# Eight instead of seven units of the down projection with seven products; where their block sums are made and loaded

## The chip, the cores and the metric

The kernel runs on one core of one Trainium2 chip. The metric is device time in microseconds, the median of several executions. The engines are TensorE (PE in the profile; its weight loads are PEld), VectorE (DVE), ScalarE (ACT), GpSimd (POOL) and SyncE (SP). Transfers between HBM and the on-chip memory are issued from the queues of SP, ACT and POOL. Three executions before the change took 295.79, 296.03 and 296.15 us, median 296.03.

## The reference

One layer of a decoder, 256 tokens of width 1024, all in float32:

```
h   = rmsnorm(x, ln1_g)
z   = h @ w_in                      # 1024 x 2824
mix = concat[pool_mixer(z), mlstm(z), attention(z)]
x   = x + mix @ w_out               # 1024 x 1024
h2  = rmsnorm(x, ln2_g)
u   = causal_dwconv3(h2 @ w_up)     # 1024 x 5632
x   = x + (silu(u[:, :2816]) * u[:, 2816:]) @ w_down   # 2816 x 1024
```

The change touches the last line. The input of the down projection, a = silu(gate) * value, has 2816 = 22 x 128 columns. The kernel takes them in 11 units of 256, so a unit is the product of a 256 x 256 part of a (tokens by columns) and a 256 x 1024 part of w_down.

## The kernel before, in words

**Precision.** Each product of float32 operands is made of three passes on TensorE. An operand is split into a high part (ScalarE copies it to the reduced type, ACT `Copy`) and a low part (VectorE subtracts the high part from the full one). Then high x high, high x low and low x high are summed in PSUM. So every block of weights costs a turn of ScalarE and a turn of VectorE before TensorE can use it.

**Units.** All weights come as units of 128 x 2048 numbers (1 MB): 11 for the input projection, 4 for the output projection, 22 for the up projection (one per pair of 128 gate and 128 value columns), 11 for the down projection (U_DOWN + 0 to 10). `load` (L187) issues a unit's transfer on SP's queue. There are four rotating buffers, and two more from the up stage on, and a transfer is issued when the low part of an earlier unit has been taken from its buffer (`load_next`, L206). High and low parts have four buffers each (HL_BUFS).

**Plain and seven-product units.** A plain down unit is 2 x 2 x 2 blocks (two token halves, two column halves of a, two halves of the 1024 outputs), three passes each: 24 matmuls of 128 x 128 x 512. The units in SEVEN (2 to 8) are computed by Strassen's scheme in Winograd's form: seven products instead of eight, 21 matmuls (`down_seven`, L1315). For it a unit needs, besides three of its four weight blocks (1536 columns, loaded as such), four sums of weight blocks (2048 columns, a second load), and four differences of blocks of a (`diffs`, L1233: three subtractions on VectorE, in place in `a_sv`). All of these are split in high and low parts too (`sums`, L1332); the differences' parts lie in `h_2`, which the up stage no longer needs (tile h in the profile). `combine` (L1369) brings the seven accumulators together at the end.

**Block sums.** The sums of weight blocks are made by the transfers themselves, in HBM (tiles `far`): for each unit three plain copies of blocks and then three transfers that add a block to what is there (`far_step`, L1216). An addition has to wait until what it adds to and what it adds has landed. All six are issued on GpSimd's queue, for one unit after the other, with the next unit's copies issued while an addition is under way (L1223 to L1231). The finished sums are loaded as a unit's second transfer. `far_gate`, a small copy on GpSimd, holds back the steps of later units until the high part of the first up unit is there.

**Order of work.** The order on each engine is written by hand. Up to the second norm a table (PLACE) sets it. In the up loop (L1246) pass i issues TensorE's matmuls of up unit i, and for ScalarE and VectorE the work on unit i - 1: `up_sum` (z), the three taps of the convolution, the gate, the split of a; between them, the split of the weight units two and three further on, and one entry of a list `late`. Its last entries are the differences of the first EARLY = 5 seven-product units; the other two units' differences are made in the down stage. After the loop the last pair's work is issued (L1388), with the preparation of the first seven-product unit between it. Then the down loop (L1406) issues the preparation of unit i + 1 or so ahead of the products of unit i. The two units LAST (9, 10) come last, in an order that lets the outputs leave early.

Of the kernel before, what the change touches and what calls it, by code (L numbers as in the profile page):

```python
# [37 lines left out]
SEVEN = (2, 3, 4, 5, 6, 7, 8)  # L38
EARLY = 5
# [101 lines left out]
def kernel(  # L141
# [42 lines left out]
    s_far, s_raw = {}, {}  # L184
    later = [(U_DOWN + i, x) for i in range(N_DOWN) for x in range(1 + (i in SEVEN))]

    def load(u, at=None):  # L187
# [16 lines left out]
        nc.sync.dma_start(raw[:, :n], src)  # L204

# [57 lines left out]
    nc.sync.dma_start(con, consts)  # L263
# [136 lines left out]
    def next_loads():  # L400
        load(RAW_BUFS - 1)
        for t in range(NT):
            nc.sync.dma_start(xs[:, t], x[t * P:(t + 1) * P])
        load(RAW_BUFS)
# [727 lines left out]
    a_hi = fpool.tile([P, NPAIR, S], F32R, name="a_hi")  # L1132
    a_lo = fpool.tile([P, NPAIR, S], F32R, name="a_lo")
# [49 lines left out]
    def up_last(i):  # L1183
        for j in range(2):
            n = 10 + 2 * i + j
            y_t[i, j] = one(f"fy{i}{j}") if i > 1 else a_sv[:, n, :]
            nc.scalar.activation(y_t[i, j], up_t[i][j], AF.Copy, scale=pcol(Q_FC + i + NPAIR * j + 4 * NPAIR))  # L1187
# [18 lines left out]
    def up_out_hi(i):  # L1206
        n = P if i in slot and i % 2 == 0 else S
        nc.scalar.activation(a_hi[:, i, :n], y_t[i, 1][:, :n], AF.Copy)  # L1208

    def up_out_lo(i):  # L1210
        n = P if i in slot and i % 2 == 0 else S
        nc.vector.tensor_sub(a_lo[:, i, :n], y_t[i, 1][:, :n], a_hi[:, i, :n].bitcast(F32))

    for i in SEVEN:
        s_far[i] = dpool.tile([P, 4, 512], F32, name=f"far{i}")
    def far_step(i, n):  # L1216
        b = w[U_DOWN + i].rearrange("p (b c) -> p b c", c=512)
        at, src, block = ((slice(0, 1), b, 0), (slice(1, 3), b, 2), (slice(3, 4), b, 1), (slice(0, 2), b, 3),
                          (slice(2, 3), s_far[i], 0), (slice(3, 4), s_far[i], 2))[n]
        nc.gpsimd.dma_start(s_far[i][:, at, :], src[:, block:block + 1, :].to_broadcast([P, at.stop - at.start, 512]),  # L1220
                            **({"accum_op": ALU.add} if n > 2 else {}))

    far_steps = [[(i, n) for n in range(3)] for i in SEVEN]  # L1223
    far_steps = [*far_steps[0], (SEVEN[0], 3), *far_steps[1], (SEVEN[0], 4), None, (SEVEN[0], 5),
                 *(x for m, i in enumerate(SEVEN) if m
                   for x in ((i, 3), *(far_steps[m + 1] if m + 1 < len(SEVEN) else ()), (i, 4), (i, 5)))]
    for x in far_steps:
        if x:
            far_step(*x)
# [16 lines left out]
    for i in range(2, NPAIR):  # L1246
        u, m = U_UP + i, i - 1
        up(i, 0)
        if i == 2:
            up_rows_t(0)  # L1250
            up_rows_t(1)
        up(i, 1)
        if i == 2:
            split(u + 2, 0)
            split(u + 2, 1)
            split_hi(u + 3, 0, 2)
            split_hi(u + 3, 1, 2)
            continue
        more = u + 3 < U_DOWN + 2
        *first, last = late.pop(0) if i > 3 and late else (None,)  # L1260
        first += [None] * (2 - len(first))
        up_sum(m)
        if more:
            split_hi(u + 3, 0, 2)
        if u + 2 < U_DOWN + 2:
            split_lo(u + 2, 0, 2)
        up_last(m)
        if more:
            split_hi(u + 3, 1, 2)
        if first[0]:  # L1270
            first[0]()
        up_taps(m)
        if m > 2:
            up_out_lo(m - 1)
        if first[1]:
            first[1]()
        up_gate(m)
        up_out_hi(m)
# [243 lines left out]
```

## Time and profile before

| | us |
|---|---|
| median of three executions | 296.03 |
| profiled execution, its own time | 295.98 |
| its span | 294.2 |
| TensorE busy | 289.6 |
| VectorE busy | 259.6 |
| ScalarE busy | 209.2 |
| GpSimd busy | 45.1 |

A row of a group gives line, engine, operation, output tile and inputs with shapes, count, busy time and mean duration, and the idle time of the engine just before. A row of a timeline gives start, length, engine, line, operation and tiles; idle time before it and what ended it stand in brackets. Times are counted from the start of the span. A row of the chain gives start, length and what ran.

### The profile page before, as it was taken

The numbers are of one execution on the slowest core, as the hardware profiler recorded it, in microseconds if no ns is written. First come the engines' busy times: TensorE is split into PE (matmuls) and PEld (weight loads), VectorE is DVE, ScalarE is ACT, GpSimd is POOL, SyncE is SP. The second block draws the span as 40 slices with busy tenths as digits, with TensorE's granted clock in tenths as the row PEclk, the third lists the DMA queues.
The fourth block names the chain that finished last, engine by engine and source line by source line (L and its number), as shares of the span: only waits on it lengthen the run. The fifth ranks groups of instructions, "written<-read, shape, count | busy, mean of one in ns | idle before, by whom it ended". The sixth has DMA issues, their size and how long they took to land.

```text
span 294.2 us, 4572 instructions
## 1 busy us (share of the span) xinstructions
PE 289.6 (98%) x1609; PEld 246.3 (84%) x1609; DVE 259.6 (88%) x518; ACT 209.2 (71%) x395; POOL 45.1 (15%) x73
## 2 busy tenths in 40 slices
PE   8999999999999999999999999999999999999995
PEld 4999888788778788888888888988988988888884
DVE  2978998999987857769999999999999989999992
ACT  3868679679894736987787787687677478786700
POOL 1000104724100005105015105015102110000000
PEclk9999999999999999999999999999999999999999
DMA  7998874079976476999998998997988988998003
GB/s 258 416 419 304 347 290 164 2 158 319 206 283 256 175 285 234 192 319 339 276 367 211 296 341 211 329 339 186 334 273 185 284 218 271 350 313 354 1 1 143
DMA packets 16599, 75.39 MB, mean 256 GB/s; under 512 B 1844, under 2 KB 2240, under 8 KB 10688
## 3 DMA queue, kind: packets, MB, share of 16 engines
q1 hardware_dynamic: 9808, 59.24, 53.7%
q0 software_dynamic: 6048, 14.68, 24.9%
q10 hardware_dynamic: 720, 1.19, 1.1%
q8 instruction: 12, 0.20, 0.3%
q14 instruction: 11, 0.09, 0.1%
HBM read 74.04 MB, written 15.73 MB: 305 GB/s over the span
## 4 chain that ended last, share of the span: by engine, by line
PE 97%; DMA 2%; DVE 0%; SPq 0%; issue 0%
PE up L1170 25%; PE up L1173 13%; PE wo L885 8%; PE dn L885 6%; PE m L1294 6%; PE dn L1294 5%; PE of L511 2%; DMA head<-in_xt 2%; PE B L497 1%; PE V L497 1%; PE V L499 1%; PE V L498 1%; PE B L499 1%; PE upr L1103 1%; PE upr L1102 1%; PE B L498 1%
## 5 line engine op out<-in xcount | busy, mean ns | idle before, releaser
L221 DVE TENSOR_TENSOR lo<-raw,hi 128x1024 fp32r<-128x1024 f32 (+2 forms) x74 | 82.7, 1136 | 2.8 <-ACT hi L214 2.8
L1170 PE MATMUL up<-h,hi 128*128 128x512 f32 x320 | 76.3, 391 | 0.0
L214 ACT ACTIVATE hi<-raw 128x1024 fp32r<-128x1024 f32 (+2 forms) x74 | 71.0, 983 | 3.1 <-PE wo L885 1.6
L1170 PEld LDWEIGHTS up<-h,hi 128*128 128x128 f32 x320 | 58.9, 188 | 11.4
L1173 PEld LDWEIGHTS up<-h,lo 128*128 128x128 f32 x320 | 41.0, 191 | 1.5
L1173 PE MATMUL up<-h,lo 128*128 128x256 f32 x320 | 41.6, 283 | 0.0
L1191 DVE SCALAR_TENSOR_TENSOR fy<-z,par,fy 128x255 f32<-128x255 f32 (+1 forms) x80 | 33.2, 478 | 0.0
L1220 POOL DMA_DIRECT2D far<-far x14 | 11.8, 846 | 106.3 <-DMA far<-in_w 57.9
L1220 POOL DMA_DIRECT2D far<-in_w x28 | 23.0, 1256 | 7.5 <-DMA far<-in_w 7.5
L1187 ACT ACTIVATE fy<-z,par 128x256 f32<-128x256 f32 x40 | 18.1, 501 | 1.5 <-DVE z L1180 1.2
L1201 ACT ACTIVATE fy<-fy 128x256 f32<-128x256 f32 x20 | 8.4, 418 | 12.0 <-DVE fy L1191 12.0
L1180 DVE TENSOR_TENSOR z<-up,zl 128x512 f32<-128x512 f32 x20 | 13.8, 689 | 3.2 <-ACT zl L1178 2.9
L1178 ACT ACTIVATE zl<-up 128x512 f32<-128x512 f32 x20 | 11.9, 595 | 4.9 <-PE up L1173 4.9
L221 DVE TENSOR_TENSOR lo<-more_raw,hi 128x1024 fp32r<-128x1024 f32 x12 | 14.6, 1217 | 0.0
L1294 PE MATMUL m<-ph,h 128*128 128x512 f32 x42 | 14.1, 389 | 0.0
L214 ACT ACTIVATE hi<-more_raw 128x1024 fp32r<-128x1024 f32 x12 | 12.6, 1052 | 0.0
L1208 ACT ACTIVATE a_hi<-a_sv 128x256 fp32r<-128x256 f32 (+1 forms) x16 | 5.7, 369 | 8.1 <-DVE a_sv L1203 8.1
L885 PE MATMUL wo<-hi,mix_hi 128*128 128x512 f32 x32 | 11.2, 411 | 0.0
L1329 ACT ACTIVATE ph<-sum 128x1024 fp32r<-128x1024 f32 x8 | 8.4, 1055 | 3.1 <-PE dn L1294 2.3
L885 PE MATMUL wo<-lo,mix_hi 128*128 128x512 f32 x32 | 10.6, 393 | 0.0
L885 PE MATMUL wo<-hi,mix_lo 128*128 128x512 f32 x32 | 10.6, 392 | 0.0
L1330 DVE TENSOR_TENSOR pl<-sum,ph 128x1024 fp32r<-128x1024 f32 x8 | 9.8, 1220 | 0.0
(331 smaller groups left out, 644.4 us busy)
## 6 DMA issues: line engine op xcount, KB each, us to landing
raw<-in_w SPq DMA_DIRECT2D x33, 1024.0 KB, 8.5
far<-in_w POOLq DMA_DIRECT2D x14, 512.0 KB, 12.2
more_raw<-in_w SPq DMA_DIRECT2D x6, 1024.0 KB, 8.7
sum<-far SPq DMA_DIRECT2D x4, 1024.0 KB, 6.9
far<-in_w POOLq DMA_DIRECT2D x14, 256.0 KB, 13.7
far<-far POOLq DMA_DIRECT2D x14, 256.0 KB, 7.2
more_raw<-far SPq DMA_DIRECT2D x3, 1024.0 KB, 8.1
raw<-in_w SPq DMA_DIRECT2D x4, 768.0 KB, 5.3
```

Of the source, the lines that this page charges most:

```text
L214: nc.scalar.activation(hi_t[u][:, s], raw_t[u][:, s], AF.Copy)
L221: nc.vector.tensor_sub(lo_t[u][:, s], raw_t[u][:, s], hi_t[u][:, s].bitcast(F32))
L885: nc.tensor.matmul(acc[t, c][:, :n], a, b[:, k, o:o + n], start=st and i == 0, stop=sp and i == 2)
L1170: nc.tensor.matmul(up_t[i][:, j], a, h_2[:, k].rearrange("p c t -> p (c t)"), start=k == 0, stop=False)
L1173: nc.tensor.matmul(up_t[i][:, j, :S], a, h_hi[:, k, :], start=False, stop=k == KT - 1)
L1178: nc.scalar.activation(zl, ps[:, :, S:], AF.Copy)
L1180: nc.vector.tensor_add(z, ps[:, :, :S], zl)
L1187: nc.scalar.activation(y_t[i, j], up_t[i][j], AF.Copy, scale=pcol(Q_FC + i + NPAIR * j + 4 * NPAIR))
L1191: nc.vector.scalar_tensor_tensor(y[:, d:], up_t[i][j][:, :S - d], pcol(Q_FC + i + NPAIR * j + 2 * NPAIR * tap), y[:, d:], op0=ALU.mult, op ...
L1220: nc.gpsimd.dma_start(s_far[i][:, at, :], src[:, block:block + 1, :].to_broadcast([P, at.stop - at.start, 512]), **({"accum_op": ALU.add} ...
L1294: nc.tensor.matmul(dst, a[x], b[y], start=start and n == 0, stop=stop and n == 2)
L1330: nc.vector.tensor_sub(l[:, s], src, h[:, s].bitcast(F32))
```

## The change

SEVEN gets unit 1, so eight units have seven products and units 0, 9 and 10 are plain. EARLY goes to 6, so that two units' differences stay in the down stage as before. The first seven-product unit's weights are now split in the last two passes of the up loop, where the plain unit 1 was split, and its sums and differences after it, in a new order of single steps.

The three copies of `far_step` for units 1 and 2 (AHEAD = 2) move to SP's queue, behind the loads of units 10 and 11 of the input and output projections. On GpSimd's queue, the additions of units 1 and 2 are issued alternately ahead of the gate; behind it come, in each round, the first addition of one unit, the second of the unit before and the third of the one before that, and then the copies of a next unit.

The constants' load moves from behind the parameters to behind unit 6's load, and the rows of x from behind unit 3's load to behind unit 14's. The tiles a_hi and a_lo leave out the 128 columns that seven-product units don't use.

```
SEVEN = (1, 2, 3, 4, 5, 6, 7, 8)        # was (2, ..., 8)
EARLY = 6                               # was 5
AHEAD = 2
...
    def load_rest(u):                   # called at the end of load(u)
        if u == 6:
            nc.sync.dma_start(con, consts)
        for i in SEVEN[:1] if u == N_IN - 1 else SEVEN[1:AHEAD] if u == N_IN else ():
            for n in range(3):
                far_step(nc.sync, i, n)
        if u == 14:
            for t in range(NT):
                nc.sync.dma_start(xs[:, t], x[t * P:(t + 1) * P])
...
    far_steps = [(SEVEN[m], n) for n in range(3, 6) for m in range(2)]
    far_steps.append(None)
    far_steps += [(SEVEN[2], n) for n in range(3)]
    for m in range(2, len(SEVEN) + 2):
        far_steps += [(SEVEN[m - n + 3], n) for n in (3, 4, 5) if 2 <= m - n + 3 < len(SEVEN)]
        if AHEAD <= m + 1 < len(SEVEN):
            far_steps += [(SEVEN[m + 1], n) for n in range(3)]
    for x in far_steps:
        if x:
            far_step(nc.gpsimd, *x)
...
    def sums(i):                        # now returns its steps by name
...
        for k in range(2):
            c = slice(768 * k, 768 * k + 768)
            add(f"w{k}", hi_t[u][:, c], lo_t[u][:, c], raw[:, c], 0 if k else None)
            c = slice(D * k, D * k + D)
            add(f"s{k}", p_hi[i][:, c], p_lo[i][:, c], s[:, c], 1 if k else None)
        add("d", *s_hl[i], a_sv[:, 2 * n:2 * n + 2, :].rearrange("p k t -> p (k t)"))
        return steps
...
    def prepare(i):
        if i in SEVEN:
            names = "w0hi w0lo w1hi w1lo s0hi s0lo dhi dlo s1hi s1lo".split()
            if SEVEN.index(i) >= EARLY:
                names = "d0 w0hi w0lo d1 w1hi w1lo d2 s0hi s0lo dhi dlo s1hi s1lo".split()
...
        def next_hi(part):              # in the up loop
            if u + 3 <= U_DOWN:
                split_hi(u + 3, part, 2)
            elif u + 3 == U_DOWN + 1:
                first[f"w{part}hi"]()
...
    m = NPAIR - 1
    up_sum(m)
    first["s0hi"]()
    first["s0lo"]()
    up_last(m)
    first["dhi"]()
    first["s1hi"]()
    up_taps(m)
    first["dlo"]()
    up_gate(m)
    up_out_hi(m)
    first["s1lo"]()
    up_out_lo(m - 1)
    up_out_lo(m)
...
    ready = 2                           # was 3
```

More of the change, by code (lines that the diff above doesn't have):

```diff
@@ L1131, with a_pair @@
     fpool = ctx.enter_context(tc.tile_pool(name="fpool", bufs=1))
-    a_hi = fpool.tile([P, NPAIR, S], F32R, name="a_hi")
-    a_lo = fpool.tile([P, NPAIR, S], F32R, name="a_lo")
+    starts, blocks_a = [], 0
+    for i in range(NPAIR):
+        starts.append(blocks_a)
+        blocks_a += 1 if i // 2 in SEVEN and i % 2 == 0 else 2
+    a_hi = fpool.tile([P, blocks_a, P], F32R, name="a_hi")
+    a_lo = fpool.tile([P, blocks_a, P], F32R, name="a_lo")
+    def a_pair(d, i):
+        return d[:, starts[i]:(starts + [blocks_a])[i + 1], :].rearrange("p b c -> p (b c)")
     a_sv = fpool.tile([P, 2 * len(SEVEN), S], F32, name="a_sv")
@@ L1206, in up_out_hi @@
     def up_out_hi(i):
-        n = P if i in slot and i % 2 == 0 else S
-        nc.scalar.activation(a_hi[:, i, :n], y_t[i, 1][:, :n], AF.Copy)
+        d = a_pair(a_hi, i)
+        nc.scalar.activation(d, y_t[i, 1][:, :d.shape[1]], AF.Copy)
     def up_out_lo(i):
[L1211 to L1226, printed above, removed]
+        h, d = a_pair(a_hi, i), a_pair(a_lo, i)
+        nc.vector.tensor_sub(d, y_t[i, 1][:, :d.shape[1]], h.bitcast(F32))
+    far_steps = [(SEVEN[m], n) for n in range(3, 6) for m in range(2)]
[5 more added lines that the diff above has]
+            far_steps += [(SEVEN[m + 1], n) for n in range(3)]
     for x in far_steps:
         if x:
-            far_step(*x)
+            far_step(nc.gpsimd, *x)
         else:
@@ L1244 @@
     late += [diffs(i) for i in SEVEN[:EARLY]]
[L1246 to L1278, printed above, removed]
-        if u + 2 < U_DOWN + 2:
-            split_lo(u + 2, 1, 2)
-        if last:
-            last()
-    assert not late
     LAST = (N_DOWN - 2, N_DOWN - 1)
@@ L1312, in down @@
                 acc[t, c] = aux([P, 512], f"dn{t}{c}")
-        rows_product(U_DOWN + i, (a_hi, a_lo), 2 * i, i == span[0], i == span[1], t, cs, sub=sub)
+        lhs = [d[:, starts[2 * i]:starts[2 * i] + 4, :].rearrange("p (k b) c -> p k (b c)", k=2) for d in (a_hi, a_lo)]
+        rows_product(U_DOWN + i, lhs, 0, i == span[0], i == span[1], t, cs, sub=sub)
     def down_seven(i):
```

109 lines of the change are left out of this document (68 added, 41 removed).

## The prediction

> **What bounds the kernel now.** I read the page first, then the chain of waits, then the stretches of the down stage, then VectorE's order of time there.
>
> ```profile
> span 294.2 us, 4572 instructions
> PE 289.6 (98%) x1609; PEld 246.3 (84%) x1609; DVE 259.6 (88%) x518; ACT 209.2 (71%) x395; POOL 45.1 (15%) x73
> ...
> PE 97%; DMA 2%; DVE 0%; SPq 0%; issue 0%
> ```
>
> TensorE carries 97% of the chain. Nothing that only starts a transfer earlier can shorten this, and fewer matmuls can, if their inputs come in time. The chain in order of time, over the down stage (start, length, what):
>
> ```profile
> 235.44 10.91 PE dn L885 x48
> 246.35 0.68 PE m L1294 x3
> ...
> 274.91 0.68 PE m L1294 x3
> ...
> 279.67 8.16 PE dn L885 x36
> ```
>
> Two plain units (0 and 1) take 10.91 us for 48 matmuls, 0.227 each. Seven units with seven products run from 246.35 to 279.67: 33.32 / 7 = 4.76 us for 21 matmuls. No wait stands between them. Next, who is nearly as busy, in the stretch of one unit (its ends, length, PE, PEld, DVE, ACT, POOL, clock, DMA share, GB/s):
>
> ```profile
> 265.40:270.10 4.70, 4.70 (x22) 3.88 (x22) 4.70 (x8) 3.89 (x5) 0.00 (x0) 1.00 1.00 417
> ```
>
> In this stretch of 4.7 us VectorE has no free time, and ScalarE has 0.8. So VectorE's order of time decides whether fewer matmuls are worth anything:
>
> ```profile
> 232.34 1.22 DVE L221 TENSOR_TENSOR lo<-raw,hi 128x1024 fp32r<-128x1024 f32 x1
> 233.48 1.66 DVE L1191 SCALAR_TENSOR_TENSOR fy<-z,par,fy 128x255 f32<-128x255 f32 x4
> 235.05 0.42 DVE L1212 TENSOR_TENSOR a_lo<-fy,a_hi 128x256 fp32r<-128x256 f32 x1
> ...
> 236.86 0.69 DVE L1180 TENSOR_TENSOR z<-up,zl 128x512 f32<-128x512 f32 x1
> ...
> 240.84 0.42 DVE L1203 TENSOR_TENSOR fy<-fy,fy 128x256 f32<-128x256 f32 x1
> 242.69 1.23 DVE L1330 TENSOR_TENSOR pl<-more_raw,ph 128x1024 fp32r<-128x1024 f32 x1 [1.44 <-ACT ph L1329]
> 243.84 0.69 DVE L277 TENSOR_TENSOR h<-a_sv,h 128x512 fp32r<-128x512 f32 x1
> 244.44 1.22 DVE L1330 TENSOR_TENSOR pl<-more_raw,ph 128x1024 fp32r<-128x1024 f32 x1
> ...
> 264.69 0.42 DVE L898 TENSOR_TENSOR a_sv<-a_sv 128x256 f32<-128x256 f32 x1
> 265.02 0.95 DVE L1344 TENSOR_TENSOR lo<-raw,hi 128x768 fp32r<-128x768 f32 x1
> 265.89 0.29 DVE L898 TENSOR_TENSOR a_sv<-a_sv 128x128 f32<-128x128 f32 x1
> 266.09 0.95 DVE L1350 TENSOR_TENSOR lo<-raw,hi 128x768 fp32r<-128x768 f32 x1
> ...
> 273.65 0.68 DVE L277 TENSOR_TENSOR h<-a_sv,h 128x512 fp32r<-128x512 f32 x1
> ...
> 287.87 0.69 DVE L1384 TENSOR_TENSOR xs<-dn,xs 128x512 f32<-128x512 f32 x1 [0.87 <-PE dn L885]
> ...
> 290.73 0.42 DVE L1384 TENSOR_TENSOR xs<-tail,xs 128x256 f32<-128x256 f32 x1 [1.01 <-PE tail L885]
> ```
>
> From start to start this gives prices on a busy VectorE: a low half of 1024 columns 1.14 us (232.34 to 233.48), of 768 0.87 (265.02 to 265.89), of 512 0.60 (243.84 to 244.44), four taps 1.57, a 256-column step 0.33 (264.69 to 265.02), a 128-column difference 0.20 (265.89 to 266.09). Preparing a unit with seven products costs 2 x 0.87 + 2 x 1.14 + 0.60 = 4.62 us, just under TensorE's 4.76. The differences of a unit add 0.33 + 2 x 0.20 = 0.73, and a unit that carries them in the down stage costs 5.35, so there VectorE falls behind by 0.59. Units 7 and 8 carry them, before and after. From 232 to 287 its only hole is the 1.44 us at 242.69. Brackets give the idle time before an instruction and what ended it.
>
> **The change, part by part.** *TensorE.* Unit 1 goes from 24 matmuls to 21: 10.91 / 48 x 3 = 0.68 us less. This is the whole gain, from inputs in time.
>
> *VectorE.* Its work ahead of the last down units grows. Removed: unit 1's split, 2 x 1.14 = 2.28. Added: unit 1 as a seven-product unit, 4.62; one more set of differences (EARLY 6, in the last pass of the up loop), 0.73. The new order of the last block (the second unit's work no longer between the gates) fills the hole: from 240.84 + 0.33 to 242.69 it was 1.52 us. It opens a small one: the last z now starts at 236.86 + 0.73 - 2 x (1.14 - 0.87) = 237.05 and ends its turn at 237.65, and the low half of the first sums then waits for its high half on ScalarE:
>
> ```profile
> 236.17 0.58 ACT L1178 ACTIVATE zl<-up 128x512 f32<-128x512 f32 x1
> 236.65 0.83 ACT L1343 ACTIVATE hi<-more_raw 128x768 fp32r<-128x768 f32 x1
> ...
> 243.09 1.05 ACT L1329 ACTIVATE ph<-more_raw 128x1024 fp32r<-128x1024 f32 x1
> ```
>
> zl moves with the gate ahead of it by 0.26 (differences 0.53 less one saved 0.27), so the high half starts at 236.17 + 0.26 + 0.48 = 236.91, ends 1.05 later, and VectorE starts at about 238.00: a hole of 0.35. Sum: 4.62 + 0.73 + 0.35 - 2.28 - 1.52 = 1.90, less some 0.05 for small holes in the old block: VectorE is 1.85 us later at unit 8.
>
> What is late then? The third product of a unit needs the low half of the differences (the 0.60 step, tile h) as weights of its third matmul. Old times on TensorE (weight loads, then a matmul):
>
> ```profile
> 276.33 0.19 PEld L1294 LDWEIGHTS dn<-hi,h 128*128 128x128 f32 x1
> ```
> ```profile
> 276.56 0.39 PE L1294 MATMUL dn<-hi,h 128*128 128x512 f32 x1
> ```
>
> Before, that low half was done at 273.65 + 0.68 = 274.33, 2.00 us ahead of the weight load at 276.33. After, it is done at 276.18, and TensorE, 0.68 earlier, would want it at 275.65: 0.53 late. How a weight load that waited is followed by its matmul is seen once, at the start (VectorE, weight load, matmul):
>
> ```profile
> 4.32 0.35 DVE L390 TENSOR_SCALAR h_f<-head 128x256 f32<-128x256 f32 x1 [4.32 <-DMA head<-in_xt]
> ```
> ```profile
> 4.73 0.96 PEld L511 LDWEIGHTS of<-head,h_f 128*128 128x128 f32 x4 [0.36 <-DVE h_f L390]
> ```
> ```profile
> 5.05 1.04 PE L511 MATMUL of<-head,h_f 128*128 128x260 f32 x4
> ```
>
> 0.06 from VectorE's end to the load, 0.32 from load to matmul, where the steady spacing is 0.23. So the matmul that started at 276.56 starts at 276.18 + 0.06 + 0.23 to 0.32 = 276.47 to 276.56. Of the 0.68 gained, 0 to 0.09 are left at this point. I take 0.09, the steady spacing, since the matmul before it still runs there. [...]
>
> Earlier units by the same chain. In unit 2 the low half of the differences follows 237.05 by the rest of the last block, 0.60 + 0.35 + 1.14 + 1.57 + 0.60 + 0.33 + 1.14 + 2 x 0.33 = 6.39 (z, the hole, first sums, taps, differences, gate, second sums, two token halves), then 1.74 + 1.14 of its own: it starts at 246.32 and is done at 247.01. Unit 8 wanted its weights at 276.33, which is 1.42 after its place 274.91 in the chain; unit 2's place is now 235.44 + 5.46 + 4.76 = 245.66, so it wants them at 247.08: 0.07 to spare, about the size of what the reading leaves open. Then VectorE gains 0.14 a unit up to unit 6 and loses 0.59 in unit 7, which comes out about even, and 0.59 in unit 8. So one stall, at unit 8. If unit 2 or 7 stalls too, unit 8's shrinks by as much, because the end is VectorE's either way. Behind it the block sums are in time: VectorE makes the first ones ahead of the differences; the second ones are done 0.60 + 1.22 - 0.69 = 1.13 later and wanted eight matmuls, 1.81, later. The tail has room for VectorE's 1.85: it waits for TensorE 0.87 us at 287.87 and 1.01 at 290.73.
>
> *Transfers.* Loads are issued by freed buffers, and in the down stage the order slips by one place.
>
> ```profile
> far<-in_w POOLq DMA_DIRECT2D x14, 512.0 KB, 12.2
> ...
> sum<-far SPq DMA_DIRECT2D x4, 1024.0 KB, 6.9
> ```
>
> The third load from here, the sums of unit 5, is the closest. It goes out when unit 2's last low half is done, 246.32 + 0.60 + 1.22 = 248.14. VectorE takes unit 5's first sums three preparations on, at 243.44 + 3 x 4.62 + 1.74 = 259.04, and ScalarE needs 1.05 before that, 258.0: 9.8 us for a landing of 6.9. Early on, the constants go behind unit 6's load (20.11), the block copies of units 1 and 2 behind those of units 10 and 11 (45.72), the x rows behind unit 14's (77.61):
>
> ```profile
> 20.11 0.33 SPq L204 DMA_DIRECT2D raw<-in_w  x1
> ```
> ```profile
> 45.72 0.33 SPq L204 DMA_DIRECT2D raw<-in_w  x1
> ```
> ```profile
> 77.61 0.33 SPq L204 DMA_DIRECT2D raw<-in_w  x1
> ```
> ```profile
> 66.34 1.04 ACT L214 ACTIVATE hi<-raw 128x1024 fp32r<-128x1024 f32 x1
> ```
> ```profile
> 239.35 0.81 POOL L1220 DMA_DIRECT2D far<-far  x1 [5.73 <-DMA far<-far]
> ```
>
> Unit 11's load at 45.72 has 20.6 us until it is used at 66.34; three copies ahead of it and three behind, at 12.2 each group, fit. The constants and the x rows are first used here:
>
> ```profile
> L558 DVE TENSOR_TENSOR gm<-gm,con x2: 416/416/417, 45.6 to 45.9; 128x256 f32<-128x256 f32 x2
> ```
> ```profile
> L895 DVE TENSOR_TENSOR xs<-wo,xs x4: 680/682/694, 104.8 to 112.5; 128x512 f32<-128x512 f32 x4
> ```
>
> From 20.11 to 45.6 and from 77.61 to 104.8 there are 25 us and more. I cost all of these at nothing, and no gain either, because TensorE waits for nothing in that part; without that cover each is worth at most one landing, 12.2. GpSimd's last add stood at 239.35; three units side by side take one wait a round where two stood, so it comes no later, against sums wanted only at about 262.
>
> Sum: -0.68 + 0.59 = -0.09. The profiled execution took 295.98 with a span of 294.2; the median is 296.03. So 296.03 - 0.09 = 295.94.
>
> **The rivals.** *A, the whole gain:* VectorE is at least 0.5 us earlier than my chain, for instance if the new block order leaves no hole (0.35) and its gate runs as early as before (0.19). Then 296.03 - 0.68 = 295.35. For it: the chain has some ten terms, each read to 0.05. Against: the rows repeat to 0.01 us from unit to unit. *B, slower:* a load lands late in the down stage. With leads down to 9.8 us, one landing of the 12.2 that the copies show is 2.4 us late on ScalarE, VectorE has no slack, and TensorE ends 2.4 us later than forecast: 298.35. It is slower than before by the bound below once a landing passes 9.8 + 0.59 + 0.09 = 10.5. For it: 417 GB/s at 265. Against: the adds then no longer run beside the loads. *C, the chain longer than figured* by 0.3 to 0.6 (a second hole in the last block): 296.25 to 296.55, still no change by the bound below.
>
> **How the numbers follow.** A measurement of this kernel tells 0.2%, 0.59 us, from no change. The forecast has 0.48, C 0.14 (both no change), A 0.24 (faster, and near the bound, so its weight is what the chain's reading leaves open), B 0.14 (slower). The likeliest alone spans 295.6 to 296.2. The range takes in A less the spread of the shown runs (0.15) below, 295.2, and C and a little of B above, 296.7; B's far end is the part left out.
>
> **What would show it.** Right: TensorE busy some 0.7 us less, one idle time of about 0.6 us before a matmul of the last seven-product unit, put down to VectorE's difference low half (tile h), VectorE without holes from 238 on. A would show no such idle time and an end 0.68 earlier. B would show ScalarE waiting for raw or sum. Wrong altogether: idle time on TensorE in the first 230 us.

## The result, and the profile after

The changed kernel takes 298.44 us (median of eight executions, 297.07 to 300.23) against 296.06 (295.79 to 296.31) for the kernel before on the same chip: a ratio of 1.0087, 95% interval 1.0063 to 1.0111. The forecast was 295.94, its range ended at 296.7: it is slower, and by none of the ways forecast. The profiled execution is the slowest of the eight (300.23), so its rows show where time went, in somewhat larger sizes than the median's 2.4 us.

The page of the changed kernel: its span, the engines' busy time, the shares of the chain.

```profile
span 298.5 us, 4590 instructions
PE 291.4 (98%) x1606; PEld 247.0 (83%) x1606; DVE 262.4 (88%) x524; ACT 210.4 (70%) x398; POOL 46.1 (15%) x73
PE 52%; DVE 31%; DMA 6%; issue 4%; ACT 4%; SPq 0%; DVEq 0%; ACTq 0%
```

Three matmuls fewer, as intended, but TensorE is no longer 97% of the chain. The chains in order of time say where. Before, then after: the first transfer, the first matmuls on it, the start of the up loop, the last step.

```profile
1.24 4.42 DMA head<-in_xt
6.36 6.40 PE of L511 x28
...
123.25 3.63 PE up L1170 x16
```
```profile
1.26 4.71 DMA head<-in_xt
6.66 6.40 PE of L530 x28
...
127.62 3.63 PE up L1197 x16
...
294.91 0.42 DVE xs L1362
```

The up loop starts 4.37 us later (127.62 against 123.25). From there to VectorE's last step the changed kernel takes 294.91 - 127.62 = 167.29, the one before 290.73 - 123.25 = 167.48: 0.19 less, where the forecast had 0.09 less. So the whole loss lies ahead of the up loop. The first matmuls start 0.30 later, behind a first transfer that took longer. The windows of the changed kernel, then of the one before (ends, length, PE, PEld, DVE, ACT, POOL, granted clock, DMA share, GB/s):

```profile
60.00:64.00 4.00, 4.00 (x20) 3.33 (x20) 3.79 (x12) 3.65 (x15) 1.54 (x2) 1.00 0.46 58
64.00:68.00 4.00, 4.00 (x20) 3.30 (x19) 3.90 (x11) 2.42 (x7) 0.00 (x0) 1.00 0.97 98
...
76.00:80.00 4.00, 2.49 (x12) 1.69 (x10) 2.92 (x5) 1.61 (x3) 0.81 (x1) 1.00 0.64 134
80.00:84.00 4.00, 3.22 (x10) 2.28 (x11) 1.89 (x14) 3.29 (x7) 0.81 (x1) 0.60 0.92 278
```
```profile
60.00:64.00 4.00, 4.00 (x20) 3.29 (x20) 3.80 (x13) 3.66 (x15) 0.90 (x2) 1.00 0.77 154
64.00:68.00 4.00, 4.00 (x19) 3.32 (x18) 3.90 (x11) 2.41 (x7) 0.00 (x0) 1.00 0.99 307
```

From 64 to 68 the transfer engines are as busy as before and move a third as much. What they carry is in GpSimd's order of time: the first additions of units 1 and 2 at 59, side by side. The next additions wait for these and start at 69.47 and 77.10, so the first ones take some 10 and 17 us.

```profile
59.05 2.49 POOL L193 DMA_DIRECT2D far<-in_w  x2
69.47 0.86 POOL L193 DMA_DIRECT2D far<-far  x1 [7.93 <-DMA far<-in_w]
77.10 0.81 POOL L193 DMA_DIRECT2D far<-far  x1 [6.77 <-DMA far<-in_w]
```

The loads of weight units 12 and 13 (output projection) go out at 61.70 and 65.66, into this. The changed kernel's chain leads through the second, 13.62 us from issue to landing:

```profile
65.66 13.62 DMA raw<-in_w
```

ScalarE in the changed kernel waits for both, where before the same steps ran at 73.96 and 75.26 with no wait:

```profile
75.48 1.06 ACT L236 ACTIVATE hi<-raw 128x1024 fp32r<-128x1024 f32 x1 [1.24 <-DMA raw<-in_w]
79.30 1.06 ACT L236 ACTIVATE hi<-raw 128x1024 fp32r<-128x1024 f32 x1 [2.39 <-DMA raw<-in_w]
```
```profile
73.96 1.07 ACT L214 ACTIVATE hi<-raw 128x1024 fp32r<-128x1024 f32 x1
75.26 1.08 ACT L214 ACTIVATE hi<-raw 128x1024 fp32r<-128x1024 f32 x1
```

ScalarE's order is fixed, so all that stands behind comes as late, and TensorE runs dry:

```profile
80.78 1.64 PE L793 MATMUL SB<-akBT,aqBT 64*128 64x128 f32 x6 [2.30 <-ACT ptsA L843]
```

2.30 us of idle time; in the window behind it the granted clock is 0.60, against 1.00 before. Matmul for matmul, the changed kernel is 0.11 us late ahead of this idle time (78.00 against 77.89) and 4.39 late at 84.67 (against 80.28), where the clock is back: 2.30 of the difference is the wait, and the other 2.0 are matmuls at the slow clock.

### The profile page after: what moved, and what is told of

The parts are those of the page before. It is cut to its first block, busy times and chain, and to the rows that moved or that the text cites. A ratio compares the mean times of both kernels' runs of the same rounds, so it can differ in the third digit from the quotient of the medians.

```text
span 298.5 us, 4590 instructions
## 1 busy us (share of the span) xinstructions
PE 291.4 (98%) x1606; PEld 247.0 (83%) x1606; DVE 262.4 (88%) x524; ACT 210.4 (70%) x398; POOL 46.1 (15%) x73
## 4 chain that ended last, share of the span: by engine, by line
PE 52%; DVE 31%; DMA 6%; issue 4%; ACT 4%; SPq 0%; DVEq 0%; ACTq 0%
PE up L1197 17%; PE up L1200 9%; DVE lo L243 8%; PE wo L904 8%; DVE pl L1321 5%; DMA raw<-in_w 5%; DVE fy L1218 4%; DVE lo L1321 3%; PE dn L904 3%; DVE a_sv L917 2%; PE of L530 2%; DMA head<-in_xt 2%; DVE z L1207 1%; PE upr L1122 1%; PE upr L1121 1%
## 5 line engine op out<-in xcount | busy, mean ns | idle before, releaser
L243 DVE TENSOR_TENSOR lo<-raw,hi 128x1024 fp32r<-128x1024 f32 (+2 forms) x72 | 80.9, 1141 | 2.9 <-ACT hi L236 2.9
L236 ACT ACTIVATE hi<-raw 128x1024 fp32r<-128x1024 f32 (+2 forms) x72 | 68.6, 980 | 8.7 <-DMA raw<-in_w 6.8
L193 POOL DMA_DIRECT2D far<-in_w x26 | 24.6, 1334 | 88.2 <-DMA far<-in_w 73.9
L193 POOL DMA_DIRECT2D far<-far x16 | 15.8, 1190 | 33.3 <-DMA far<-in_w 19.8
L1276 PE MATMUL m<-ph,h 128*128 128x512 f32 x48 | 16.1, 389 | 0.0
L1235 ACT ACTIVATE a_hi<-a_sv 128x256 fp32r<-128x256 f32 (+1 forms) x18 | 6.4, 368 | 9.1 <-DVE a_sv L1230 9.1
L1321 DVE TENSOR_TENSOR pl<-sum,ph 128x1024 fp32r<-128x1024 f32 x10 | 12.2, 1223 | 0.0
L917 ACT ACTIVATE ph<-sum 128x1024 fp32r<-128x1024 f32 x10 | 10.5, 1048 | 1.1 <-DMA sum<-far 0.7
L904 PE MATMUL wo<-lo,mix_hi 128*128 128x512 f32 x32 | 10.6, 393 | 0.0
L904 PE MATMUL wo<-hi,mix_lo 128*128 128x512 f32 x32 | 10.6, 392 | 0.0
```

Of the source, the lines that this page charges most:

```text
L193: queue.dma_start(s_far[i][:, at, :], src[:, block:block + 1, :].to_broadcast([P, at.stop - at.start, 512]), **({"accum_op": ALU.add} if n ...
L236: nc.scalar.activation(hi_t[u][:, s], raw_t[u][:, s], AF.Copy)
L243: nc.vector.tensor_sub(lo_t[u][:, s], raw_t[u][:, s], hi_t[u][:, s].bitcast(F32))
L904: nc.tensor.matmul(acc[t, c][:, :n], a, b[:, k, o:o + n], start=st and i == 0, stop=sp and i == 2)
L917: return lambda: f(*a)
L1276: nc.tensor.matmul(dst, a[x], b[y], start=start and n == 0, stop=stop and n == 2)
```

## The experiments

Theory S: two additions in flight together slow the loads beside them, and the loads of units 12 and 13 have no lead (time from issue to first use) to spare. It explains the rows above; the runs were to shake it. The runs were on several chips; each ratio is against the kernel before on the same chip, where that takes 296.06 to 296.14. In the diffs, plus lines replace or join the changed kernel's.

### Where the early wait comes from

**The early additions behind the gate.**

```
-    far_steps = [(SEVEN[m], n) for n in range(3, 6) for m in range(2)]
-    far_steps.append(None)
+    far_steps = [None, *((SEVEN[m], n) for n in range(3, 6) for m in range(2))]
```

> The changed kernel with one edit: the six additions of units 1 and 2 are issued behind GpSimd's gate (from about 112 us) instead of ahead of it (from 59 us). The copies of these units stay on SP's queue, the constants and x rows stay where the change put them. Theory S (two additions side by side fill the DMA engines from 60 to 77 us and make the loads of units 12 and 13 land late): these loads land in 8 to 9 us, ScalarE waits for raw under 1 us there, TensorE has no idle time at 78 us, and the time is 4.3 - 0.3 us less than the profiled changed kernel, 295.9. Rival Q (what SP's queue took on, the block copies, delays the loads): the idle time at 78 us stays at 2 us or more and the time at 298 to 299. Both expect the wait of some 0.5 us at unit 8 for the low half of the differences.

311.22 us, ratio 1.0475 (1.0442 to 1.0508). The early wait is gone, but the block sums come too late. The waits (us in total, times, longest):

```profile
PE dn L1275 <- ACT h L917: 11.9, 1, 11.9
...
ACT ph L917 <- DMA sum<-far: 15.8, 3, 14.3
```

**Only unit 1's three ahead of the gate.**

```
+    far_steps = [(SEVEN[0], n) for n in range(3, 6)] + [None] + [(SEVEN[1], n) for n in range(3, 6)]
```

> The changed kernel with one edit: only unit 1's three additions stay ahead of the gate, one after the other; unit 2's go behind it. Theory S with the number of additions in flight as the cause: one addition at a time takes half of what two take, the load of unit 12 lands 3 to 5 us earlier than in the changed kernel and the load of unit 13 within 10 us, so TensorE's idle time at 78 us is under 0.3 us and the time is 295.9 to 296.3. If any addition in flight with these loads is enough, the idle time stays over 1 us and the time over 297. Rival Q: 298 to 299.

305.67, ratio 1.0331 (1.0290 to 1.0371). Again no early wait; the last addition goes out at 263.91 and TensorE waits 7.7 us in the down stage. So the early additions make the early loss, and they are also needed: behind the gate a round of additions takes some 16 to 26 us, and what is not done ahead is missed at the end.

**The copies back on GpSimd's queue**, ahead of the side-by-side additions (`far_step` is left out of `load_rest`):

```
+    far_steps = [(SEVEN[m], n) for n in range(6) for m in range(2)]
```

> The changed kernel with one edit: the six block copies of units 1 and 2 leave SP's queue and are issued on GpSimd's, ahead of their additions, which stay side by side ahead of the gate. Theory S: more transfers meet the loads of units 12 and 13 on the DMA engines than before, so the wait of ScalarE for raw stays or grows, 298 to 301 us. Rival Q: SP's queue holds loads alone again, so the wait is gone and the time is 295.9.

303.80, ratio 1.0258 (1.0243 to 1.0274). TensorE waits 3.5 us before the output projection and 1.0 before the attention's matmuls, the sums are in time (last addition at 249.46). The time is above the 298 to 301 that S had expected, but of its kind: the loss follows the additions to where they now run, and the copies on SyncE's queue are not its cause.

**Eight units with the transfers of before** (all on GpSimd's queue, in the old order; constants and x rows at their old places):

> The eighth seven-product unit with the old transfers: SEVEN from 1 to 8, the new order on VectorE, but all copies and additions on GpSimd in the old order, the constants and x rows at their old places. Theory S and the prediction's sum: no idle time on TensorE before 230 us, one wait of about 0.5 us at unit 8 for the low half of the differences, 295.9 us. If the block sums of eight units come too late in the old order, ScalarE waits for sum and the time is over 297. If the eighth unit itself cost the time: 298 to 299.

313.70, ratio 1.0595 (1.0556 to 1.0635); the last addition goes out at 281.04. The old order, with the sums at this place, does not carry an eighth unit.

### One addition at a time

```
+    far_steps = [(SEVEN[m], n) for m in range(2) for n in range(3, 6)]
```

> The changed kernel with the six early additions in another order on GpSimd's queue: the three of unit 1 one after the other, then the three of unit 2, all still ahead of the gate. Same bytes, same instructions, same queue; never two additions in flight together early. Theory S (two additions in flight slow the loads of units 12 and 13, and one alone does not): ScalarE waits for raw at 74 to 80 us not at all or under 0.5 us, TensorE loses neither the 2.30 us wait nor the slow clock behind it, the block sums come in time, and the time falls by some 2.4 to 3 us to 295.4 to 296.2. Theory V (it is the number of early additions, six bytes-heavy transfers, and not that they run side by side): the wait stays, time 297.5 to 299.

299.06, ratio 1.0089 (1.0054 to 1.0124). The wait at 80 us is gone, as S has it, and the loss is not: TensorE now waits 2.8 us before the output projection. This run's windows, GpSimd and ScalarE:

```profile
60.00:64.00 4.00, 4.00 (x20) 3.34 (x20) 3.83 (x13) 3.67 (x14) 0.52 (x1) 1.00 0.57 54
64.00:68.00 4.00, 4.00 (x19) 3.33 (x18) 3.86 (x12) 2.40 (x7) 0.00 (x0) 1.00 0.96 107
```
```profile
76.47 1.48 POOL L193 DMA_DIRECT2D far<-in_w  x1
88.19 0.85 POOL L193 DMA_DIRECT2D far<-far  x1 [10.24 <-DMA far<-in_w]
```
```profile
102.97 2.00 ACT L236 ACTIVATE hi<-raw 128x1024 fp32r<-128x1024 f32 x2 [6.06 <-DMA raw<-in_w]
```

One addition alone holds the engines at 54 and 107 GB/s, as two did. Unit 2's now runs from 76 to 88 and makes later loads late. So S is wrong in its "two together": a single addition is as slow, and what it costs depends on which load it meets.

**The same, and in the down units the differences' halves ahead of the sums:**

```
-            names = "w0hi w0lo w1hi w1lo s0hi s0lo dhi dlo s1hi s1lo".split()
+            names = "w0hi w0lo w1hi w1lo dhi dlo s0hi s0lo s1hi s1lo".split()
...
-                names = "d0 w0hi w0lo d1 w1hi w1lo d2 s0hi s0lo dhi dlo s1hi s1lo".split()
+                names = "d0 w0hi w0lo d1 w1hi w1lo d2 dhi dlo s0hi s0lo s1hi s1lo".split()
```

> As the run with the six early additions one after the other, and in each down unit the differences' high and low half (tile h) made ahead of the two halves of the block sums rather than between them. If the wait at the eighth unit is what the prediction's chain made it (the low half of the differences some 0.5 us late, the block sums with over a microsecond to spare), TensorE's wait there (0.46 us in the changed kernel) goes and the time is 0.4 to 0.5 us below that of the other run, about 295.2 to 295.6. If instead VectorE's total is the bound whatever the order (then the block sums are late in their turn), the wait moves to the block sums (tile ph or pl) and the time stays.

302.40, ratio 1.0194 (1.0170 to 1.0219). The wait for tile h is gone, and two waits for tile pl are there (0.29 and 0.75 us, units 7 and 8): in this order VectorE stands still 0.70 us in each of them for ScalarE's high half of the differences. The early loss is in it too.

**Constants and x rows back at their old places**, all else as changed:

> The changed kernel with the load of the constants and the loads of the x rows issued where the kernel before issues them (the constants behind the parameters at the start, the x rows between the two loads ahead of the attention); the block copies and the additions as in the changed kernel. Theory S: the wait of TensorE at about 80 us stays, time within 0.6 us of the changed kernel, 297.8 to 299. Rival R (the moved constants or x rows collide with the loads of units 12 and 13): the wait goes, 295.6 to 296.2.

298.94, ratio 1.0109 (1.0079 to 1.0138): the loss stays, so it is not theirs.

### What is slow: the adding, or the bytes?

**Plain copies in place of the early additions.** The sums of units 1 and 2 are left out by this.

```
-                        **({"accum_op": ALU.add} if n > 2 else {}))
+                        **({"accum_op": ALU.add} if n > 2 and i not in SEVEN[:2] else {}))
```

> The changed kernel in which the early transfers of units 1 and 2 on GpSimd's queue that add (six) are plain copies of the same bytes and the same places, still two side by side; the additions of these two units are left out. Theory S1 (it is the adding transfer that is slow, some 10 to 17 us for two of 0.25 or 0.5 MB, and takes the engines' time): the copies land in under 6 us, the loads of units 12 and 13 land in under 10 us, no wait of ScalarE for raw at 74 to 80 us, time 295.6 to 296.2. Theory S2 (it is the bytes or the number of queues, whatever the transfers do): the wait stays, time 297.5 to 299.

296.14, ratio 1.0000 (0.9991 to 1.0008): all of the loss is gone. From 64 to 68 the transfer engines move 302 GB/s here, where the changed kernel has 98, and GpSimd's order of time shows the second unit's transfer done 1.2 us behind the first's, not 7.6:

```profile
68.28 0.56 POOL L193 DMA_DIRECT2D far<-far  x1 [7.29 <-DMA far<-in_w]
69.50 0.54 POOL L193 DMA_DIRECT2D far<-far  x1 [0.67 <-DMA far<-in_w]
```

So it is the adding. The value is also near the forecast's 295.94, whose sum has no slow additions in it.

**The changed kernel's transfers with seven units** (the kernel before, with `load_rest` and the new `far_steps`; units 2 and 3 are the early ones):

> The kernel before with seven units, and the changed kernel's transfers alone: constants, x rows and the copies of the first two units with seven products (here 2 and 3) on SyncE's queue where the changed kernel has them, their six additions side by side ahead of the gate, three units side by side behind it. Theory S (the six early additions make the loads of units 12 and 13 late, whatever the down stage does): ScalarE waits for raw at 74 to 80 us by some 3.5 us, TensorE waits at about 80 us, time 297.8 to 299.5, no wait at the last unit. Rival U (the loss needs the eighth unit): 295.8 to 296.3.

295.92, ratio 0.9996 (0.9987 to 1.0005). I had expected the loss here too. Six additions of the same sizes, issued at the same times, cost nothing, and in this run's window and GpSimd's rows they are faster:

```profile
64.00:68.00 4.00, 4.00 (x20) 3.30 (x18) 3.86 (x13) 2.25 (x6) 0.63 (x1) 1.00 0.97 215
```
```profile
67.37 0.86 POOL L193 DMA_DIRECT2D far<-far  x1 [5.54 <-DMA far<-in_w]
74.05 0.81 POOL L193 DMA_DIRECT2D far<-far  x1 [5.82 <-DMA far<-in_w]
```

215 GB/s against 98. The two kernels differ here in what is added (units 2 and 3, not 1 and 2) and perhaps in where the sums lie: if weights and sums lie unit behind unit, 1 MB each, and the sums begin at the same place, then with one unit more the distance from a sum to its weights differs by a megabyte. No trace shows the addresses.

### Where the sums lie in memory

Theory M: how fast an addition runs hangs on the place of its target against its source.

**A megabyte ahead of the sums, eight units:**

```
+    unused = dpool.tile([P, 2048], F32, name="unused")
+    nc.gpsimd.dma_start(unused[:1, :16], w[0][:1, :16])
     for i in SEVEN:
         s_far[i] = dpool.tile([P, 4, 512], F32, name=f"far{i}")
```

> The changed kernel with an unused tile of one megabyte in memory ahead of the block sums (and one transfer of 64 bytes at the start that writes to it), so that all sums lie a megabyte further on; nothing else differs. Theory M (how fast an adding transfer runs depends on where its target lies against its source): the early additions take another time than the 10 and 17 us of the changed kernel, and the time leaves 297.1 to 300.2; if this distance is a good one, 295.6 to 296.4. Rival N (it is not the place): as the changed kernel, 297.1 to 300.2, with TensorE's wait at about 80 us.

308.43, ratio 1.0388 (1.0340 to 1.0437): 10 us more than the changed kernel for a change of place. It comes elsewhere than expected. The early additions are as slow as in the changed kernel and no slower (the next ones start at 69.40 and 77.39), and the up loop starts at 124.88. But from there to VectorE's last step it takes 177.47 us, against 167.29: the rounds of additions behind the gate take 23 to 28 us and not 17 to 24, the last addition goes out at 267.36 and not at 243.96, and the down units wait for sums.

```profile
267.36 0.80 POOL L195 DMA_DIRECT2D far<-far  x1 [7.66 <-DMA far<-far]
```

**Rows of the sums 8448 bytes apart in place of 8192:**

```
-        s_far[i] = dpool.tile([P, 4, 512], F32, name=f"far{i}")
+        s_far[i] = dpool.tile([P, 2112], F32, name=f"far{i}")[:, :2048].rearrange("p (b c) -> p b c", c=512)
```

> The changed kernel with the rows of the block sums 8448 bytes apart in memory in place of 8192, so that no row of a sum lies at the same distance from its row of weights as the next. Theory M (conflicts between source and target at a fixed distance): the early additions land in under 8 and 14 us, no wait of TensorE at 80 us, 295.6 to 296.4. Rival N: as the changed kernel, 297.1 to 300.2; rows of another pitch cannot help if the additions are slow by themselves.

296.06, ratio 0.9998 (0.9988 to 1.0007). Same instructions, same bytes, same queues as the changed kernel, and its loss is gone. Window and GpSimd's rows of this run:

```profile
64.00:68.00 4.00, 4.00 (x20) 3.30 (x19) 3.90 (x11) 2.42 (x7) 0.07 (x1) 1.00 1.03 185
```
```profile
67.93 0.86 POOL L193 DMA_DIRECT2D far<-far  x1 [6.32 <-DMA far<-in_w]
73.31 0.81 POOL L193 DMA_DIRECT2D far<-far  x1 [4.53 <-DMA far<-in_w]
```

The two additions are through at 68 and 73, not 69 and 77. ScalarE still waits for the load of unit 13, 0.77 us in place of 2.39, but TensorE no longer does. The second addition is through at 73.31 to 74.72 in all four profiles with another pitch (this one and three below), and at 76.88 to 77.39 in the changed kernel, the run with constants and x rows back and the one with the megabyte. This run and the one with the megabyte were on the same chip.

**A megabyte ahead of the sums, seven units:**

> The run with seven units and the changed kernel's transfers, with an unused megabyte ahead of the block sums, which gives units 2 and 3 the places in memory that the changed kernel gives them. Theory M: the early additions slow down to the changed kernel's 10 and 17 us, ScalarE waits for raw at 74 to 80 us, time 297 to 299. Rival N: as without the megabyte, 295.7 to 296.6.

297.02 (295.72 to 298.27), ratio 1.0026 (1.0007 to 1.0045). Slower by 1.1 us than without the megabyte, and just within the time that M had expected. What M had expected of the additions did not come in the profiled execution (295.83): they are through at 66.29 and 74.35, about as without the megabyte, the load of unit 13 is 0.81 us late for ScalarE, and no matmul waits. So this trace does not bear out that the distance alone makes the changed kernel's additions slow. What stands of M is that the place decides: on one chip, eight units took 308.43 and 296.06 with the same instructions (but for one transfer of 64 bytes at the start of the first) and the sums at other places. Whether it is the distance, the place itself or the pitch is open.

### An earlier gate

```
+    far_gate = cpool.tile([P, 1], F32, name="far_gate")
...
+    far_steps = [(SEVEN[0], n) for n in range(3, 6)] + [None] + [(SEVEN[1], n) for n in range(3, 6)]
...
-            nc.gpsimd.tensor_copy(upool.tile([P, 1], F32, name="far_gate"), hi_t[U_UP][:, 2047:2048].bitcast(F32))
+            nc.gpsimd.tensor_copy(far_gate, hi_t[U_UP][:, 2047:2048].bitcast(F32))
```

> The changed kernel with the three early additions of unit 1 ahead of the gate, unit 2's behind it (as in the run with one unit ahead), and the gate's one-element copy written to a tile of its own that is free from the start, so that the gate waits for the first up unit's high half alone (at about 101 us) and no longer for memory that the attention's tiles leave at 111. All additions behind the gate start some 10 us earlier. Theory S (an addition in flight makes the loads beside it late, and the last sums are late by the time behind the gate): no idle time on TensorE before 100 us; if the loads of the first up units (used at 109 to 119 us) have the lead to bear one addition, the last addition is at 252 to 255 us, the last sums are in time or under 1 us late, and the time is 295.8 to 297. If those loads have no lead, TensorE waits at 105 to 125 us and the time is 298 or more.

300.56, ratio 1.0156 (1.0124 to 1.0189). The gate opens at 102.13 and no matmul waits before the down stage, but unit 2's first addition starts 9.3 us earlier than in the run with one unit ahead (102.63 against 111.95) and the last addition of all only 6.5 (257.38 against 263.91), and ScalarE waits 5.2 us for sums. At the slow place, each spot tried for unit 2's additions costs time, early or at the end.

**The same with the differences made early in units 7 and 8:**

```
+                names = "d0 d1 w0hi w0lo d2 w1hi dhi w1lo dlo s0hi s0lo s1hi s1lo".split()
```

> As the run with the gate ten us earlier, and in the last two units the differences' steps made early (d0, d1, then the first low half, d2, then tile h's high half right behind the second high half of the weights, its low half ahead of the block sums). If VectorE's low half of the differences at the eighth unit is the only thing that takes back the gain there (0.46 us in the changed kernel) and the block sums have some 0.1 us to spare, the wait at the eighth unit goes and the time is 0.3 to 0.5 us below the other run's; best case 295.4. If the block sums are late in their turn, the wait moves to a matmul that waits for tile pl, and the time stays within 0.2 us of the other run's.

302.37, ratio 1.0204 (1.0175 to 1.0233). The sums are late as in the run before, so this says nothing on the order, except that the waits in units 7 and 8 are now for tile pl (0.23 and 0.35 us).

### What the eighth unit is worth

**Plain copies again (units 1 and 2's additions left out), with that order:**

> As the run with plain copies in place of units 1 and 2's additions (these additions are left out), with the order of the last two units of the run with the gate earlier and the new order. Without any stall early, this shows the eighth unit's worth by itself: 0.68 us of TensorE less 0 to 0.1 us, so 295.4 to 295.6 if the order frees the low half of the differences, 296.1 if the block sums are late in its place.

296.61, ratio 1.0013 (1.0004 to 1.0022), 0.47 slower than with the changed kernel's order. TensorE's one wait is for the low half of the first sums, and VectorE twice waits 0.18 us for ScalarE:

```profile
277.29 0.50 PE L1276 MATMUL m<-pl,h 128*128 128x512 f32 x1 [0.35 <-DVE pl L1321]
```

**The pitch of 8448, and the differences of units 7 and 8 on GpSimd**, free from 240 on:

```
+        e = nc.vector if SEVEN.index(i) < EARLY else nc.gpsimd
+        return [do(e.tensor_sub, v[:, 0:2], v[:, 1:2].to_broadcast([P, 2, P]), v[:, 0:4:3]),
...
```

> The run with rows of another pitch (8448 bytes), and the differences d0, d1, d2 of the last two units (7 and 8) on GpSimd, whose last addition is issued at about 240 us and which is free from there. VectorE is spared 2 x 0.73 us. If VectorE's time is what holds the low half of the differences back at the eighth unit (and not ScalarE or a transfer), no matmul of the down units waits for tile h or pl, and the time is 0.4 to 0.5 us below the pitch run's 296.06: 295.5 to 295.7, faster than the kernel before by about 0.15%. If GpSimd takes more than about 3 us for a unit's three steps, or slows VectorE beside it, the wait stays or grows: 296.0 to 296.6.

297.88, ratio 1.0059 (1.0046 to 1.0072): slower. GpSimd's six steps in this run, VectorE's four taps beside them, and the same taps in the run with the pitch alone:

```profile
239.60 4.57 POOL L917 TENSOR_TENSOR a_sv<-a_sv 128x256 f32<-128x256 f32 x6
```
```profile
239.33 3.68 DVE L1218 SCALAR_TENSOR_TENSOR fy<-z,par,fy 128x255 f32<-128x255 f32 x4
```
```profile
239.29 1.66 DVE L1218 SCALAR_TENSOR_TENSOR fy<-z,par,fy 128x255 f32<-128x255 f32 x4
```

VectorE loses 2.02 us on the taps alone to save 1.46 later, and loses them just ahead of units 1 and 2 (the prediction had found 0.07 to spare at unit 2): TensorE waits there 1.01 and 0.54 us for tile h. The wait at unit 8 is gone.

**The same with rows 10240 bytes apart:**

> As the run with the differences on GpSimd, with rows 10240 bytes apart in place of 8448. Theory M in its general form (any pitch that is not that of the weights spreads the additions): no wait of TensorE at 80 us, the same time as the other run within 0.2 us. If 8448 is a lucky place: TensorE waits at 80 us again, 297 to 299.

297.95, ratio 1.0069 (1.0056 to 1.0083), 0.07 from the other, with no wait at 80 us: 8448 is not a single lucky pitch. Here GpSimd's six steps are spread over 31.95 us, and TensorE waits for tile h at 272 (1.04 us) and not in units 1 and 2, so that the two times agree so closely is in part chance.

**The pitch of 8448, and VectorE's holes closed:**

```
-                names = "d0 w0hi w0lo d1 w1hi w1lo d2 s0hi s0lo dhi dlo s1hi s1lo".split()
+                names = "d0 d1 d2 w0hi w0lo w1hi dhi w1lo dlo s0hi s0lo s1hi s1lo".split()
...
     up_sum(m)
+    up_out_lo(m - 1)
     first["s0hi"]()
...
     first["s1lo"]()
-    up_out_lo(m - 1)
     up_out_lo(m)
```

> The run with rows of another pitch (8448 bytes), and VectorE's order changed in two places. In the last block of the up stage the low half of the output before last (0.33 us) goes into the hole of 0.25 us behind the last z. In units 7 and 8 the three differences come first, tile h's high half right behind the second high half of the weights and its low half ahead of the block sums, so that ScalarE has the differences early and VectorE finds no hole of 0.18 us at the first sums. In the run with copies and the other order the first low half of the sums of unit 8 was 0.51 us late (276.55 to 277.29 where 0.23 is steady); 0.25 + 2 x 0.18 = 0.61 us is closed here, so it is in time by 0.1. If VectorE's time is the only thing in the way: no wait of TensorE at units 7 and 8, time 0.4 to 0.5 us below the pitch run's 296.06, so 295.5 to 295.7. If the second low half of the weights (0.03 us late there) or another product takes over: 295.8 to 296.2.

296.04 (295.32 to 297.13), ratio 1.0000 (0.9991 to 1.0010). The mechanism came as expected and the time did not. In the profile TensorE waits for nothing from 7 us to the tail. The chain of this run:

```profile
1.26 4.77 DMA head<-in_xt
6.73 6.41 PE of L530 x28
...
123.56 3.63 PE up L1197 x16
...
290.54 0.42 DVE xs L1362
```

From the up loop's start to the last step it takes 290.54 - 123.56 = 166.98, 0.50 less than before. But its first matmuls start 0.37 later (6.73 against 6.36), because the head lands later, and the span ends 3.76 us behind that last step, where before it was 3.47: that makes 294.3, against 294.2. In the profiles in whose chain it stands the head took 4.35 to 4.88 us; of the kernel before there is one profile. Whether the later head comes with the change or with the run is open, and so is why the median shows nothing of the 0.50. No version beat the kernel before.

## Why the prediction was wrong

**The step that failed is "I cost all of these at nothing ... because TensorE waits for nothing in that part".** The transfers step looked at unit 11's load, at the constants and at the x rows, and priced the moved copies at a landing of 12.2. What moved forward with the copies was not priced: the additions that had stood behind them on GpSimd's queue now start at 59, beside two loads, of which the second has a lead of 9.8 us (unit 13, out at 65.48, used at 75.26 before). The row for this was in the trace: before, three copies went out at 58.90 and the first addition only at 68.40. What the runs showed in place of nothing: beside the additions that load took 13.62 us, TensorE stood for 2.30 us and then ran at a clock of 0.60, and the kernel lost 2.4 us in the median. With copies in place of these additions (296.14), or with another row pitch (296.06), the loss is gone. That idle time on TensorE in the first 230 us would prove the forecast "wrong altogether" was the right sign, and it came.

The price of 12.2 was misread too: its row counts all transfers of 512 KB on GpSimd's queue, in each unit one copy and one addition, so it isn't what "the copies show".

Could the size have been known? Not exactly, since it hangs on where the sums lie (308.43 and 296.06 on one chip). A bound could: the kernel before, too, has windows in which the transfer engines are full and move little while additions run. GpSimd's rows there (the second issues an addition of 512 KB), and the window:

```profile
222.38 0.83 POOL L1220 DMA_DIRECT2D far<-far  x1 [9.86 <-DMA far<-far]
222.93 1.48 POOL L1220 DMA_DIRECT2D far<-in_w  x1
```
```profile
224.00:228.00 4.00, 4.00 (x21) 3.35 (x20) 4.00 (x9) 3.25 (x6) 0.41 (x1) 1.00 0.99 125
```

125 GB/s, where 64 to 68 had 307. An estimate from these rows: the loads of units 12 and 13, 2.1 MB together, need 16.8 us at 125 GB/s, and from 61.54 to 75.26 they had 13.7, so some 3 us late, where ScalarE's step came 4.0 later (79.30 against 75.26). So the step was wrong in that it gave no bound for a new overlap of additions and loads. With the sums' rows at another pitch its answer, nothing, is what was measured (296.06 against the forecast's 295.94).

**GpSimd's last addition "comes no later".** It goes out at 243.96 against 239.35, but the gate had opened 4.38 later (115.93 against 111.55): counted from the gate it is 0.23 later, so this was right but for the early loss.

**TensorE's 0.68 and the wait at unit 8: right, sizes a little off.** The forecast had one wait, in front of the third product's third matmul in unit 8, for tile h. It is TensorE's only wait in the down stage. VectorE's low half, then the weight load and the matmuls of the changed kernel:

```profile
242.37 1.23 DVE L1321 TENSOR_TENSOR pl<-more_raw,ph 128x1024 fp32r<-128x1024 f32 x1 [0.25 <-ACT ph L917]
...
279.87 0.68 DVE L1321 TENSOR_TENSOR h<-a_sv,h 128x512 fp32r<-128x512 f32 x1
```
```profile
280.60 0.19 PEld L1276 LDWEIGHTS dn<-hi,h 128*128 128x128 f32 x1 [0.61 <-DVE h L1321]
```
```profile
280.02 0.39 PE L1276 MATMUL dn<-lo,h 128*128 128x512 f32 x1
280.61 0.50 PE L1276 MATMUL dn<-hi,h 128*128 128x512 f32 x1 [0.19 <-DVE h L1321]
280.94 0.40 PE L1276 MATMUL m<-ph,h 128*128 128x512 f32 x1
```

The hole in VectorE's last block is 0.25 (forecast 0.35). But it ends where the forecast has it: 242.37 is 238.00 and the 4.37 by which the up loop starts later. So VectorE's chain came out as worked out, and its low half at unit 8 is done at 280.55, which is 276.18 and 4.37. The matmul would stand at 280.25 in steady spacing and the next at 280.48; they start at 280.61 and 280.94, so the wait costs 0.46 (forecast 0.59). 0.68 - 0.46 = 0.22, and the down part shows 0.19. The term that was too dear is the step from weight load to matmul, 0.23 to 0.32: here it is 0.01 (280.60 to 280.61), in a load whose row is 0.19 long; but the next matmul then comes 0.33 later in place of 0.23, so part of it is paid there.

**Rival A (no stall, the whole gain)** asked for VectorE to be 0.5 us earlier. The last run gave it about that and got 0.50 in the down part, not 0.68, and nothing in the median. **Rival B** had the right kind (a load too late for ScalarE, its order fixed, TensorE behind it) but in the down stage, where ScalarE waits once, 0.74 us, for a sum and TensorE not behind it; that its 298.35 is nearly the time is luck. The mechanism was looked for only where leads had shrunk, and not where new traffic had come. **Rival C** did not occur: no second hole.

## What to carry to other kernels

When a change lets a transfer start earlier, price what it now runs beside, not only whether it lands in time: list each load in flight then with its lead, and bound the slowdown by the bytes per second of the slowest window that the trace shows. A transfer that adds in memory is not to be priced as a copy of the same size: here the engines moved 98 GB/s with the early additions and 302 with copies in their place, and with the sums at other places eight units took 308.43, 298.44 and 296.06, so try another row pitch before rearranging queues. And reordering an engine that has hardly a hole gave nothing back here (296.61 against 296.14 with copies, 296.04 against 296.06 with the other pitch): work must leave it, and to an engine that doesn't slow it down, as GpSimd did (four taps 3.68 us in place of 1.66).

## What the hardware showed

- Adding transfers between two places in HBM, with 128 rows at a pitch of 8192 bytes on both sides: one of 512 KB, with loads beside it, took some 10.6 and 11.7 us in the run with one addition at a time (59.20 to 69.77, 76.47 to 88.19), and from 60 to 68 us the transfer engines moved 54 and 107 GB/s (125 in the kernel before, from 224 to 228). With the sums' rows 8448 bytes apart they moved 185 from 64 to 68, where the changed kernel has 98. An unused megabyte ahead of the sums cost 10 us (308.43 against 298.44), through the additions behind the gate. Plain copies in place of six of the additions cost nothing (296.14). With 256 bytes more a row (8448) the loss was gone (296.06 against 298.44), and with 2048 more (10240) no matmul waited at 80 us either.
- VectorE beside GpSimd: four taps of 1.66 us took 3.68 while GpSimd ran differences in SBUF (239.33, pitch 8448); in the run with rows 10240 bytes apart, where GpSimd's differences begin at 242.93, the taps at 239.68 took 1.66. GpSimd's six steps took 4.57 us in the first of these runs and 31.95 in the other.
- The clock: behind an idle time of 2.30 us (the changed kernel, 80.78) the granted clock was 0.60 over four microseconds, 80 to 84; behind one of 1.35 us (the run with constants and x rows back) it stayed at 1.00:

```profile
80.08 0.92 PE L791 MATMUL SB<-akBT,aqBT 64*128 64x128 f32 x6 [1.35 <-ACT ptsA L841]
```
```profile
80.00:84.00 4.00, 3.92 (x22) 3.10 (x23) 2.59 (x14) 3.97 (x11) 1.22 (x2) 1.00 0.94 267
```
